# One gate's modulation computed among the FFN's products, and the residual stream loaded step by step

## The chip, the cores and the metric

The kernel runs on one core of a Trainium2 chip. The metric is the device time of one execution in microseconds (us): the median of a few executions, here 2656.18 us over three (2654.99 to 2662.91). The core has five engines with queues of their own: TensorE (PE in the profile; PEld is its loading of weights), VectorE (DVE), ScalarE (ACT), GpSimd (POOL) and SyncE (SP), which here only issues transfers. Each runs its queue in order and waits on semaphores for the others. Transfers issued by SyncE and by GpSimd go to the same 16 DMA engines.

## The reference

One layer of a hybrid decoder for 512 prompt tokens and 8 single new tokens, model width 2048, in float32. Cut to what matters:

```
mod = silu(c) @ w_ada + b_ada                       # 6 x 2048 columns
sh1, sc1, gt1, sh2, sc2, gt2 = split(mod, 6)
h = rmsnorm(x, g_norm_mix) * (1 + sc1) + sh1
q, k, v, p_rwkv = split(h @ w_in)
att = banded_attention(q, k, v)                     # window 128, ALiBi, sinks
rw, S, last = rwkv7_mix(p_rwkv, ...)                # delta-rule recurrence, 16 heads
x = x + gt1 * (concat(att, rw) @ w_out)
h2 = rmsnorm(x, g_norm_ffn) * (1 + sc2) + sh2
gate, up = split(h2 @ w_ffn_in)                     # hidden width 5632
x = x + gt2 * ((silu(gate) * up) @ w_ffn_out)
y = rmsnorm(x, g_norm_final)
```

Besides y it returns the last 128 key and value rows of the prompt, the recurrent states, the last projection row, and for the new tokens the key and value caches shifted by one row with the new row at the end. The caches hold 8 x 128 rows of 256 numbers each (1 MB a cache).

## The kernel before

**Numbers.** Activations lie transposed, features on the 128 partitions, and all 520 tokens as two halves of 260 columns. A float32 product is done as three: each weight and each activation is split into a high part that the fast matmul type holds exactly and the rest, and high x high, high x low and low x high are summed (`mm3`, line 98). Weights come in units of 128 x 512 (256 KB): SyncE issues the load (`raw`, line 86), ScalarE casts the high part (`wh`, line 88), VectorE subtracts (`wl`, line 91). In the FFN's first stage the like is done in lines 1269 and 1270.

**Stages.** (1) Startup: norm and first modulation. (2) Input projection: 39 tiles `pm`, each 16 steps of six matmuls of 260 columns, with the RWKV recurrence running between them. Of it only the chain matters here: for each pair of heads the prompt goes through 32 half-steps, each one small matmul group into `psc` from the state `Z`, then a step on VectorE and one on ScalarE that write `Z` anew, before the next can start. The pair's output follows (`pY`, its group norm, the gate `pg`, then `V` stored to `catd` in device memory). (3) Query, key and value tiles of the projection are written to device memory and read back for attention. (4) The concatenated activations are read back (`catl` from `catd`, line 1349, two buffers), split, and the output projection runs: `wout_part(0, 8)` over the first 8 of 16 steps of the contraction, which needs no attention output and makes 16 tiles `po` of 48 matmuls while attention runs between them, then `wout_part(8, 12)`, then the last four steps half by half with the second norm. (5) FFN, first stage (`ffn_in`): 44 tiles of hidden width in a scheme of seven products in place of eight (line 1439), with sums of weights made by accumulating transfers on GpSimd's queue. (6) FFN, second stage (`pf`, line 98), last norm, results (line 1602).

**Modulation.** `ada_gen` (line 304) computes the gates and shifts GT1, SH2, SC2 and GT2 while stage 2 runs. Each is 64 groups: SyncE loads 256 KB of `w_ada` into `ar` (three buffers), and TensorE multiplies it in four column tiles of 32 x 128 (line 314). After every 16 groups the result is copied by ScalarE, transposed and added to the bias.

**Order.** The order of instructions comes from two places. Background jobs are generators (`ada_gen`, the recurrence, attention, loads), and `pump()`, called after each step of six matmuls in the main tiles, advances those whose time has come in a small model clock (0.62 a call; `spent` adds what a job's own instruction takes). A scheduler then lays the instructions out on each engine.

**Residual stream.** `x_load` loads the input x again into eight tiles of two feature blocks each (`x1[0]` to `x1[7]`), on which `accumulate` (line 1193) adds GT1 times an output tile, on VectorE. `new_kv_sample` copies the 127 kept rows of the two caches from device memory to device memory on GpSimd's queue, after the first store of key rows.

Of the kernel before, what the change touches and what calls it, by code (L numbers as in the profile page):

```python
# [7 lines left out]
F32 = mybir.dt.float32  # L8
F32R = mybir.dt.float32r
AF = mybir.ActivationFunctionType  # L10
ALU = mybir.AluOpType
# [3 lines left out]
P = 128  # L15
KD = 16
T = 512
NS = 8
HB = 260
# [8 lines left out]
SH1, SC1, GT1, SH2, SC2, GT2 = 0, 16, 32, 48, 64, 80  # L28
# [35 lines left out]
class Kern:  # L64
    def __init__(self, tc, I, O, upto="all"):
        self.tc, self.nc, self.I, self.O, self.upto = tc, tc.nc, I, O, upto
        self.n = 0
        self.bg = []
        self.free, self.done_at = {}, 0.0
        self.px = PacedCore(self)  # L70
        self.nada = 0
        self.sample_done = self.kv_done = self.decode_done = False
        self.cat_out, self.cat_in = set(), 0
        self.psc = None
        self.squares, self.pending = [None, None], None

# [72 lines left out]
    def run(self):  # L149
        tc, nc, I = self.tc, self.nc, self.I  # L150
        R = dict(side="right")
        with ExitStack() as st:
# [15 lines left out]
            with ExitStack() as st2:  # L168
# [33 lines left out]
                with tc.tile_pool(name="ap", bufs=1, **R) as self.ap:  # L202
                    self.attn_phase()
                    self.wout_part(0, 8)
                    self.wout_part(8, 12)
                    self.drain()
# [97 lines left out]
    def ada_gen(self):  # L304
        nc = self.px
        for c in (GT1, SH2, SC2, GT2):
            for q in range(4):
# [508 lines left out]
    def x_load(self):  # L816
        for i in range(8):
            src = self.I["x"]
            for a, b in ((0, 1), (1, 2)) if i == 0 else ((0, 2),):
                (self.nc.sync if i else self.nc.gpsimd).dma_start(self.x1[i][:, a:b], src[:, 2 * i + a:2 * i + b])  # L820
            if i in (1, 2, 3, 5, 7):
                self.done_at += 4
                yield

# [22 lines left out]
    def kv_gen(self):  # L847
# [9 lines left out]
        for gp in range(2):  # L857
# [4 lines left out]
            yield  # L862
        self.first_kv = self.nc.gpsimd.dma_start(O["kp"], self.Kt[:, :, 384:512])
        nc.gpsimd.dma_start(O["vp"], self.Vt[:, 3])
# [3 lines left out]
    def new_kv_sample(self):  # L868
        nc, I, O, ap = self.px, self.I, self.O, self.ap
        with self.tc.issue_after(self.first_kv.ins):  # L870
            for n in ("k", "v"):
                self.nc.gpsimd.dma_start(O[n + "s"][:, 0:127, :], I["cache_" + n][:, 1:128, :])
        pt = self.aux("ptx")
# [487 lines left out]
    def wout_part(self, k0, k1):  # L1361
# [4 lines left out]
        for o in range(KD):  # L1366
            ps = self.ps_m.tile([P, 2, 512], F32, tag="m", name=self.nm("po"))
            for kk in range(n):
# [4 lines left out]
                self.pump()  # L1373
            self.accumulate(o, ps, GT1)

    def wout_half(self, h, kept):
# [23 lines left out]
    def ffn_in(self, st):  # L1400
# [45 lines left out]
        def finish(ht, pc, cu):  # L1446
# [7 lines left out]
            yield  # L1454

        norm = self.norm_second(lambda nm: mt(nm)[:, 0])
        early = len(self.pcd)
# [15 lines left out]
        for i, ht in enumerate(order):  # L1473
# [4 lines left out]
            else:  # L1478
                p12 = mt("pm")
            p45, p67, p3 = mt("pm"), mt("pm"), mt("pm")  # L1480
            for g in range(2):
                a11, a21 = load(ht, 0, 0, g), load(ht, 1, 0, g, places[(2 * i + g) % 4])
                a22 = load(ht, 1, 1, g, "raw")
# [18 lines left out]
                for ps, a, b in ((p45[:, 1], a21, T1), (p67[:, 0], a11, T2), (p67[:, 1], s3, T3),  # L1502
                                 (p45[:, 0], a22, T4), (p3[:, 0], a12, B22)):
                    product(ps, weights(a), b, g)
                    if b is T1:
                        if old and g:
                            nc.vector.tensor_tensor(s3, a11, a22, ALU.subtract)
                        nc.vector.tensor_tensor(a12, a12, a11, ALU.add)
                        next(rest, None)
# [78 lines left out]
    def last_block(self, b, g):  # L1588
# [39 lines left out]
        r = self.norm(1, mt("ssq3")[:, 0], nc)  # L1628
        for eng, o in ((nc.vector, 0), (nc.gpsimd, 8), (nc.vector, 2), (nc.gpsimd, 10), (nc.vector, 4), (nc.vector, 6),
                       (nc.gpsimd, 14), (nc.vector, 12)):  # L1630
            result(eng, 1, r, o, 2)

# [108 lines left out]
```

## Time and profile before

| | |
|---|---|
| median of 3 executions | 2656.18 us (2654.99 to 2662.91) |
| the profiled execution | 2657.76 us, of which the span 2656.0 us |
| TensorE busy | 2554.5 us, 96% of the span |
| VectorE, ScalarE, GpSimd busy | 1723.8, 1105.9, 382.5 us |
| moved by DMA | 460 MB, 173 GB/s mean |
| last projection tile ends, output projection begins | 926.7 us |
| FFN, first and second stage | the stretch 1262 to 2124 lies in the first; the second from 2130 us |

The span is what the profiler sees of one execution; the device time is a little longer. A timeline row gives start, duration, engine, line, operation, output<-input and count, and in brackets the idle time before it with what released it. A row of a group gives busy time and mean duration in ns, and then the idle time before its instructions. A row of a stretch gives its length, then busy time (and instructions) of PE, PEld, DVE, ACT and POOL, then the granted clock of TensorE (1.00 is full), the busy share of the DMA engines and GB/s. A row of transfers gives count, KB of each, and the median time from issue to landing.

### The profile page before, as it was taken

Reading aid. Unit: us, or ns where it says so; the run is one execution under the profiler, and the core shown is the slowest. Engines: PE = TensorE matmul, PEld = TensorE weight load, DVE = VectorE, ACT = ScalarE, POOL = GpSimd, SP = SyncE. Lnnn points to the kernel's source line nnn. Section 1 sums busy time; section 2 is a strip of 40 time slices with the busy share of each in tenths; the row PEclk is TensorE's granted clock in tenths of the full one; section 3 lists DMA queues with packets and bytes.
Section 4 is the critical chain, followed back from the end, with each engine's and each line's share of the span. In section 5 each row is a group of like instructions: output and inputs, shape, how many; then the busy total and the mean of one; then the engine's idle time right before and its main releaser. Section 6 shows DMA issues by size and latency. Waiting matters only on the chain. (4 is left out here: it accounts for less than half of the span.)

```text
span 2656.0 us, 59166 instructions
## 1 busy us (share of the span) xinstructions
PE 2554.5 (96%) x23373; PEld 2340.7 (88%) x23373; DVE 1723.8 (65%) x3880; ACT 1105.9 (42%) x2153; POOL 382.5 (14%) x525
## 2 busy tenths in 40 slices
PE   7899999999999999998999999999999999999997
PEld 4677777888787889898999999999999999999997
DVE  5466767777657444678777777777777763444456
ACT  3133444545533324547544444444444532222225
POOL 0012112112112000021111212111121100000004
PEclk9999999999989999999999999999999999999999
DMA  9855445455546675245777777777777552333333
GB/s 347 294 165 154 152 126 162 149 166 160 159 153 207 203 251 146 94 160 183 191 201 204 193 208 198 191 207 198 194 208 200 155 184 92 124 125 102 116 105 106
DMA packets 241704, 460.22 MB, mean 173 GB/s; under 512 B 32353, under 2 KB 44561, under 8 KB 241393
## 3 DMA queue, kind: packets, MB, share of 16 engines
q1 hardware_dynamic: 206880, 379.88, 44.5%
q0 software_dynamic: 33904, 75.50, 13.4%
q8 instruction: 183, 3.00, 0.5%
q10 hardware_dynamic: 640, 1.05, 0.2%
q14 instruction: 97, 0.79, 0.1%
HBM read 421.73 MB, written 35.59 MB: 172 GB/s over the span
## 5 line engine op out<-in xcount | busy, mean ns | idle before, releaser
L88 ACT CAST wh<-raw 128x512 fp32r<-128x512 f32 (+2 forms) x410 | 246.9, 606 | 510.5 <-PE pf L98 278.9
L98 PE MATMUL pf<-go,wh 128*128 128x260 f32 x2560 | 414.1, 281 | 0.0
L91 DVE TENSOR_TENSOR wl<-raw,wh 128x512 fp32r<-128x512 f32 (+2 forms) x410 | 283.8, 694 | 200.4 <-ACT wh L88 194.8
L98 PEld LDWEIGHTS pf<-go,wh 128*128 128x128 f32 x2560 | 354.0, 188 | 0.1
L98 PE MATMUL pm<-hH,wh 128*128 128x260 f32 (+1 forms) x1248 | 301.3, 319 | 7.3 <-ACT wh L88 6.7
L1269 ACT CAST wh<-sr 128x512 fp32r<-128x512 f32 x320 | 198.1, 621 | 261.7 <-PE pm L1439 232.0
L1270 DVE TENSOR_TENSOR wl<-sr,wh 128x512 fp32r<-128x512 f32 x320 | 220.6, 690 | 83.0 <-ACT wh L1269 75.9
L98 PE MATMUL pm<-hH,wl 128*128 128x260 f32 (+1 forms) x1248 | 265.4, 292 | 5.2 <-DVE wl L91 5.1
L98 PE MATMUL pf<-go,wl 128*128 128x260 f32 x1280 | 267.7, 282 | 0.0
L1439 PE MATMUL pm<-xT,wh 128*128 128x260 f32 x1408 | 263.2, 286 | 4.4 <-DVE pc L1516 4.3
L98 PE MATMUL pm<-hL,wh 128*128 128x260 f32 (+1 forms) x1248 | 263.4, 291 | 0.0
L1439 PE MATMUL pm<-T,wh 128*128 128x260 f32 x1408 | 257.6, 283 | 0.0
L98 PEld LDWEIGHTS pm<-hH,wh 128*128 128x128 f32 (+1 forms) x1248 | 196.5, 191 | 57.8 <-issue 31.6
L1439 PEld LDWEIGHTS pm<-xT,wh 128*128 128x128 f32 x1408 | 216.9, 188 | 11.0 <-DVE pc L1516 6.1
L1439 PEld LDWEIGHTS pm<-T,wh 128*128 128x128 f32 x1408 | 216.9, 188 | 0.0
L98 PEld LDWEIGHTS pm<-hH,wl 128*128 128x128 f32 (+1 forms) x1248 | 197.4, 192 | 16.0 <-DVE wl L91 8.7
L1439 PE MATMUL pm<-B0H,wl 128*128 128x260 f32 x704 | 201.4, 286 | 9.6 <-DVE wl L1270 9.1
L98 PEld LDWEIGHTS pm<-hL,wh 128*128 128x128 f32 (+1 forms) x1248 | 196.9, 191 | 7.5 <-issue 5.2
L1439 PE MATMUL pm<-B0H,wh 128*128 128x260 f32 x704 | 200.3, 285 | 2.0 <-DVE acct L1206 1.7
L98 PEld LDWEIGHTS pf<-go,wl 128*128 128x128 f32 x1280 | 200.9, 188 | 0.0
L1439 PE MATMUL pm<-B0L,wh 128*128 128x260 f32 x704 | 198.9, 282 | 0.0
L1439 PE MATMUL pm<-T,wl 128*128 128x260 f32 x704 | 198.7, 282 | 0.0
(427 smaller groups left out, 5243.8 us busy)
## 6 DMA issues: line engine op xcount, KB each, us to landing
ar<-in_w_ada SPq DMA_DIRECT2D x256, 256.0 KB, 3.1
sr<-in_w_fi SPq DMA_DIRECT2D x176, 256.0 KB, 4.6
raw<-in_w_fo SPq DMA_DIRECT2D x176, 256.0 KB, 2.6
raw<-in_w_in SPq DMA_DIRECT2D x144, 256.0 KB, 3.7
araw<-in_w_ada SPq DMA_DIRECT2D x64, 512.0 KB, 6.5
raw<-in_w_fi SPq DMA_DIRECT2D x120, 256.0 KB, 4.6
s<-in_w_fi SPq DMA_DIRECT2D x80, 256.0 KB, 4.4
s<-in_w_fi POOLq DMA_DIRECT2D x80, 256.0 KB, 5.1
```

The costliest lines, as they stand in the source:

```text
L88: nc.scalar.copy(wh[:, :n], raw[:, :n])
L91: nc.vector.tensor_tensor(wl[:, :n], raw[:, :n], wh[:, :n].bitcast(F32), ALU.subtract)
L98: nc.tensor.matmul(ps[:m, bank, :HB], w, a[:, k, h, :], start=first and i == 0, stop=last and i == 2, skip_group_check=True,)
L1269: nc.scalar.copy(H, src)
L1270: nc.vector.tensor_tensor(L, src, H.bitcast(F32), ALU.subtract)
L1439: nc.tensor.matmul(ps[:, :HB], x[:, s], y, start=g == k == i == 0, stop=g == 1 and k == 3 and i == 2, skip_group_check=True)
```

## The change

Four edits.

1. `ada_gen` leaves GT2 out. Its 64 groups move into the FFN's first stage: in iterations 11, 18, 25 and 32 of 44, 16 groups each, four groups after each of two products (those with T2 and T4), in both halves of the contraction, into the free bank of `p3`. The loads stand at the iteration's halves, into tiles of a pool of 12. GT2 is used in the FFN's second stage only.
2. `x_load` puts tile 0 on GpSimd's queue, tiles 1 and 2 on SyncE's, and tiles 3 to 7 on GpSimd's, each behind a copy of one element from the x tile three places before it, which waits until the output tiles of that one have been accumulated.
3. The cache copies move from the first key store to behind the last x load, by the program between `wout_part(0, 8)` and `wout_part(8, 12)`.
4. The last eight multiplies of results go all to VectorE; before, three were GpSimd's.

```diff
@@ the program @@
                     self.wout_part(0, 8)
+                    with tc.issue_after(self.last_x.ins):
+                        for n in ("k", "v"):
+                            nc.gpsimd.dma_start(self.O[n + "s"][:, 0:127, :], I["cache_" + n][:, 1:128, :])
                     self.wout_part(8, 12)
@@ ada_gen @@
-        for c in (GT1, SH2, SC2, GT2):
+        for c in (GT1, SH2, SC2):
@@ x_load @@
-                (self.nc.sync if i else self.nc.gpsimd).dma_start(self.x1[i][:, a:b], src[:, 2 * i + a:2 * i + b])
-            if i in (1, 2, 3, 5, 7):
-                self.done_at += 4
-                yield
+                self.last_x = (self.nc.sync if 0 < i < 3 else self.nc.gpsimd).dma_start(self.x1[i][:, a:b], src[:, 2 * i + a:2 * i + b])
+            if i < 2:
+                continue
+            self.done_at += 4
+            yield
+            if i < 7:
+                while self.cat_o < 2 * (i - 2) + 2:
+                    yield
+                nc = self.nc
+                nc.gpsimd.tensor_copy(self.x1[i + 1][:, 0, 0, 0:1], self.x1[i - 2][:, 1, 1, 259:260])
@@ new_kv_sample @@
-        with self.tc.issue_after(self.first_kv.ins):
-            for n in ("k", "v"):
-                self.nc.gpsimd.dma_start(self.O[n + "s"][:, 0:127, :], I["cache_" + n][:, 1:128, :])
@@ wout_part, after each output tile @@
             self.accumulate(o, ps, GT1)
+            self.cat_o += 1
@@ ffn_in @@
+        def ada(ps, q, g, j):
+
+            for k in range(8 * g + 4 * j, 8 * g + 4 * j + 4):
+                for c in range(4):
+                    nc.tensor.matmul(ps[32 * c:32 * c + 32, 0:128], self.cT[:, k, :], self.pieces[0][:, c * 128:(c + 1) * 128], start=k == 0, stop=k == KD - 1,
+                                     tile_position=(0, 32 * c), skip_group_check=True)
+                self.pieces.pop(0)
+            if k < KD - 1:
+                return
+            res = self.fp.tile([P, 2, HB], F32, tag="n", bufs=self.nb, name=self.nm("adar"))[:, 0, 0:128]
+            nc.scalar.copy(res, ps[:, 0:128])
+            nc.tensor.transpose(ps[:, 128:256], res, self.ident)
+            f0 = GT2 + 4 * q
+            nc.vector.tensor_tensor(
+                self.mod[:, f0:f0 + 4, :], ps[:, 128:256].rearrange("p (f t) -> p f t", f=4)[:, :, 0:9],
+                self.par[:, P_BA + f0:P_BA + f0 + 4].unsqueeze(2).broadcast_to([P, 4, 9]), ALU.add)
+
+        def ada_load(q, g):
+            for k in range(8 * g, 8 * g + 8):
+                t = self.fp.tile([P, 2, HB], F32, tag="n", bufs=self.nb, name=self.nm("ar"))
+                t = t.rearrange("p a t -> p (a t)")[:, 0:512]
+                nc.sync.dma_start(t, I["w_ada2"][12 + q, k])
+                self.pieces.append(t)
...
+            q = (11, 18, 25, 32).index(i) if i in (11, 18, 25, 32) else None
             for g in range(2):
+                if q is not None:
+                    ada_load(q, g)
...
                     product(ps, weights(a), b, g)
+                    if q is not None and (b is T2 or b is T4):
+                        ada(p3[:, 1], q, g, b is T4)
@@ last_block @@
-        for eng, o in ((nc.vector, 0), (nc.gpsimd, 8), (nc.vector, 2), (nc.gpsimd, 10), (nc.vector, 4), (nc.vector, 6),
-                       (nc.gpsimd, 14), (nc.vector, 12)):
-            result(eng, 1, r, o, 2)
+        for o in range(0, KD, 2):
+            result(nc.vector, 1, r, o, 2)
```

Since the background jobs go by the model clock, taking 64 groups out shifts what stands behind them. Three places of the order of instructions show it. In the changed file the lines of helpers are one to seven further down.

TensorE, at the end of the last pair's recurrence. Before, the pair's output `pY` stands among the matmuls of a projection tile, with groups of `ada` between them, and more projection tiles follow:

```order
L49 MATMUL psc<-Z_1733,LS_1738 64x64 x2
L98 MATMUL pm_11127<-hH,wh_11180 128x260 x2
L98 MATMUL pm_11127<-hL,wh_11180 128x260 x2
L98 MATMUL pm_11127<-hH,wl_11181 128x260 x2
L314 MATMUL ada_11012<-ar_11168,cT 32x128 x4
L98 MATMUL pm_11127<-hH,wh_11180 128x260 x2
L98 MATMUL pm_11127<-hL,wh_11180 128x260 x2
L98 MATMUL pm_11127<-hH,wl_11181 128x260 x2
L49 MATMUL pY_11203<-Z_1733,RR_9364 32x64 x10
L314 MATMUL ada_11012<-ar_11196,cT 32x128 x4
L49 MATMUL pY_11203<-Z_1733,RR_9364 32x64 x22
L98 MATMUL pm_11127<-hH,wh_11180 128x260 x2
```

With the change the projection tiles have run out here. The last of them ends, and the recurrence goes on alone: `psc` reads the state `Z`, `L` and `LS` are the two kinds of half-step.

```order
L99 MATMUL pm_10921<-hH,wh_11027 128x260 x2
L99 MATMUL pm_10921<-hL,wh_11027 128x260 x2
L99 MATMUL pm_10921<-hH,wl_11028 128x260 x2
L49 MATMUL psc<-Z_1733,L_1218_8537 32x64 x2
L49 MATMUL pYx_11082<-cst,ys 64x64 x2
L49 MATMUL pY_11174<-Z_1733,RR_9381 32x64 x9
L49 MATMUL psc<-Z_1733,LS_1738 64x64 x2
L49 MATMUL pY_11174<-Z_1733,RR_9381 32x64
L49 MATMUL psc<-Z_1733,L_1218_8537 32x64 x2
L49 MATMUL pY_11174<-Z_1733,RR_9381 32x64
L49 MATMUL psc<-Z_1733,LS_1738 64x64 x2
L49 MATMUL pY_11174<-Z_1733,RR_9381 32x64
```

From the first `psc` row here 24 half-steps of the pair's 32 stand one behind the other, each with a piece of `pY` in between; no projection tile is left to stand among them, and before the first `po` come only small matmuls (decode attention, `pt`, `pg`, transposes, first logits).

SyncE, around the store of the last pair's output (`catd_87`) and the loads of the concatenated activations (`catl`). Before:

```order
L49 DMA catd_87<-V_9369 128x512
L49 DMA ar_11402<-in_w_ada 128x512
L463 DMA qd_105<-sp_11366 128x512
L49 DMA ar_11424<-in_w_ada 128x512
L1349 DMA catl_11394<-catd_80 128x512
L1349 DMA catl_11416<-catd_81 128x512
L49 DMA ar_11452<-in_w_ada 128x512
L86 DMA raw_11582<-in_w_in 128x512
L86 DMA raw_11614<-in_w_in 128x512
L1349 DMA catl_11444<-catd_82 128x512
L86 DMA raw_11646<-in_w_in 128x512
L1349 DMA catl_11466<-catd_83 128x512
```

With the change:

```order
L49 DMA catd_87<-V_9386 128x512
L49 DMA q_11657<-qd_100 128x512
L49 DMA q_12014<-qd_101 128x512
L1356 DMA catl_11246<-catd_80 128x512
L1356 DMA catl_11250<-catd_81 128x512
L49 DMA q_12310<-qd_102 128x512
L49 DMA q_12599<-qd_103 128x512
L1356 DMA catl_11254<-catd_82 128x512
L1356 DMA catl_11258<-catd_83 128x512
L1356 DMA catl_11262<-catd_84 128x512
L1356 DMA catl_11266<-catd_85 128x512
L49 DMA bias_12312<-in_alibi 128x2x256
```

The store stands ahead of the `catl` loads in both. Before, `ar` and projection weights stand among them, and tiles of the projection run beside them; with the change there are neither, and the first units of `w_out` are loaded ahead of the store. Seven x loads came behind these rows on SyncE before; now five of the eight tiles stand on GpSimd's queue, the cache copies behind them.

TensorE, in the FFN's first stage, iteration 11 (`T_1` is the last operand of a product, `ar` the loaded modulation weights):

```order
L1447 MATMUL pm_18271<-T_1_14708,wh_18353 128x260 x2
L1447 MATMUL pm_18271<-T_1_14708,wl_18354 128x260
L1468 MATMUL pm_18272<-ar_18273,cT 32x128 x4
L1468 MATMUL pm_18272<-ar_18275,cT 32x128 x4
L1468 MATMUL pm_18272<-ar_18277,cT 32x128 x4
L1468 MATMUL pm_18272<-ar_18279,cT 32x128 x4
L1447 MATMUL pm_18271<-xT_14995,wh_18385 128x260 x2
L1447 MATMUL pm_18271<-xT_14995,wl_18386 128x260
```

Four groups of four small matmuls each stand between two products that stood next to each other before.

More of the change, by code (lines that the diff above doesn't have):

```diff
@@ L74, in __init__ @@
         self.psc = None
+        self.cat_o = 0
         self.squares, self.pending = [None, None], None
@@ L862, in kv_gen @@
             yield
-        self.first_kv = self.nc.gpsimd.dma_start(O["kp"], self.Kt[:, :, 384:512])
+        nc.gpsimd.dma_start(O["kp"], self.Kt[:, :, 384:512])
         nc.gpsimd.dma_start(O["vp"], self.Vt[:, 3])
@@ L869, in new_kv_sample @@
         nc, I, O, ap = self.px, self.I, self.O, self.ap
-        with self.tc.issue_after(self.first_kv.ins):
-            for n in ("k", "v"):
-                self.nc.gpsimd.dma_start(O[n + "s"][:, 0:127, :], I["cache_" + n][:, 1:128, :])
         pt = self.aux("ptx")
@@ L1454, in finish @@
             yield
+        def ada(ps, q, g, j):
[19 more added lines that the diff above has]
+                self.pieces.append(t)
+        self.pieces = []
         norm = self.norm_second(lambda nm: mt(nm)[:, 0])
```

## The prediction

> **What bounds the kernel now.** I read the page's head first, then busy time by stage, then the rows of the two places that the change touches. First the head.
>
> ```profile
> span 2656.0 us, 59166 instructions
> PE 2554.5 (96%) x23373; PEld 2340.7 (88%) x23373; DVE 1723.8 (65%) x3880; ACT 1105.9 (42%) x2153; POOL 382.5 (14%) x525
> ```
>
> TensorE is busy 96% of the span, so its own work and the few places where it waits decide. Busy time in four stretches (last columns: granted clock, DMA share, GB/s): the last part of the in-projection, the first two output-projection tiles, the attention with the tiles after them, the FFN's first stage.
>
> ```profile
> 724.00:926.80 202.80, 196.79 (x1996) 161.36 (x1995) 116.76 (x260) 68.49 (x157) 28.81 (x22) 0.96 0.60 190
> 926.80:938.30 11.50, 11.50 (x98) 11.50 (x98) 3.88 (x15) 2.25 (x4) 2.71 (x5) 1.00 0.97 295
> 938.30:992.00 53.70, 47.77 (x426) 46.01 (x426) 24.78 (x71) 15.96 (x37) 3.55 (x6) 0.94 0.68 244
> 1262.00:2124.00 862.00, 850.88 (x6978) 840.74 (x6977) 644.82 (x1118) 402.96 (x673) 163.27 (x206) 1.00 0.75 196
> ```
>
> TensorE idles 6 us in the first (first two columns), none in the second, 5.9 in the third, 11 of 862 in the fourth. Work moved into the FFN therefore costs nearly its full time, and work taken from the in-projection pays only if TensorE has something else to do there.
>
> **Removed from the in-projection.** The 64 groups of GT2 lie in the first stretch; its groups of instructions, and what TensorE waited for:
>
> ```profile
> L314 PE MATMUL ada<-ar,cT 128*32 128x128 f32 x512 | 28.3, 289 | 3.9 <-DMA ar<-in_w_ada 3.8
> L49 PE MATMUL psc<-Z,LS 128*64 128x64 f32 x124 | 10.8, 254 | 0.5 <-ACT Z L49 0.3
> ...
> L49 PE MATMUL pg<-SG,lf 128*128 128x512 f32 x12 | 4.0, 427 | 0.0
> L49 PE MATMUL pY<-Z,RR 128*32 128x64 f32 x128 | 2.7, 222 | 0.0
> ```
>
> One such group between two others:
>
> ```profile
> 708.44 0.41 PE L98 MATMUL pm<-hL,wh 128*128 128x260 f32 x2
> 708.68 0.40 PE L98 MATMUL pm<-hH,wl 128*128 128x260 f32 x2
> 709.02 0.43 PE L314 MATMUL ada<-ar,cT 128*32 128x128 f32 x8
> 709.27 0.28 PE L49 MATMUL psc<-Z,L 128*32 128x64 f32 x4
> ```
>
> A pair of projection matmuls normally takes 0.24 us (708.44 to 708.68). Here the group starts 0.34 after the pair, so 0.10 late, and holds the queue 0.25. At least 64 x 0.35 + 3.8 of waiting = 26 us goes. At most it is all busy time and idle time, 32.2, plus 64 x 0.10 = 39 us. I take 36.5, near the top, since most groups stand between projection matmuls and delay those behind them too.
>
> **What takes its place.** By the order of instructions, the projection tiles now run out with 24 of the last pair's 32 chain half-steps still to come; before, they ran between these tiles. A half-step goes TensorE, VectorE, ScalarE, TensorE; two of them (projection rows left out):
>
> ```profile
> 849.45 0.34 PE L49 MATMUL psc<-Z,LS 128*64 128x64 f32 x4
> ...
> 849.91 0.28 DVE L49 TENSOR_SCALAR Z<-psc,PC 64x64 f32<-64x64 f32 x1 [0.84 <-PE psc L49]
> ...
> 850.22 0.31 ACT L49 ACTIVATE Z<-psc,PC 64x64 f32<-64x64 f32 x1 [0.91 <-DVE Z L49]
> ...
> 850.75 0.31 PE L49 MATMUL psc<-Z,L 128*32 128x64 f32 x4
> 850.78 0.62 ACT L88 CAST wh<-raw 128x512 fp32r<-128x512 f32 x1 [0.25 <-PE pm L98]
> ...
> 851.17 0.23 DVE L49 COPY Z<-psc 32x64 f32<-32x64 f32 x1 [0.99 <-PE psc L49]
> ...
> 851.44 0.21 ACT L49 COPY Z<-psc 32x64 f32<-32x64 f32 x1
> ```
>
> The LS step ends its round at 850.53 (850.22 + 0.31) and the L step at 851.65, so 1.0 to 1.3 us each, mean near 1.13; under other work a half-step cost TensorE some 0.45 (its own 0.25 and the disturbed pairs about it). Moving 24 of them out of the stretch shortens it by 24 x 0.45 = 10.8. Some 4 us of the pair's other matmuls move too: half of the 2.7 of pY, four pg at 0.43, four pt at about the 0.3 of other matmuls. The last projection tile thus ends at 926.7 - 36.5 - 10.8 - 4 = 875.4.
>
> From there 24 x 1.25 = 30 us of chain with TensorE almost idle. I take 1.25 rather than 1.13 because of the clock. Behind tiny matmuls, and again behind a stall, it falls (third-last column):
>
> ```profile
> 778.00:784.00 6.00, 6.00 (x33) 5.00 (x33) 2.12 (x14) 1.86 (x6) 0.00 (x0) 0.50 0.33 108
> ...
> 948.00:954.00 6.00, 2.30 (x10) 2.30 (x11) 1.42 (x4) 0.62 (x1) 0.94 (x2) 0.67 1.02 410
> 954.00:960.00 6.00, 6.00 (x42) 6.00 (x41) 2.08 (x3) 2.06 (x4) 0.14 (x1) 0.77 0.73 238
> 960.00:966.00 6.00, 6.00 (x52) 6.00 (x52) 2.40 (x6) 1.49 (x3) 0.00 (x0) 1.00 0.72 230
> ```
>
> At half clock the 0.31 to 0.34 us of matmul become some 0.13 longer. The Trainium skill speaks against the change here ("TensorE: Matmul & The Clock Gate", Part 1: The HAM clock gate): the array gets half its clock after an idle window of about 3.4 us and full clock only after as long a sustained run. The 0.67 and 0.77 above agree, standing behind a stall of 4.29 us quoted below. By the rule the whole exposed chain and the first products behind it run at half clock, and 24 x 1.13 = 27 us of chain would be 30; by the rows' own pace 27.
>
> Then the pair is normalised and written; the last step, the multiply that ends it, the store, and what loads and stores take to land over the run (last column):
>
> ```profile
> 886.71 0.27 DVE L49 TENSOR_SCALAR L<-psc,PC 64x64 f32<-64x64 f32 x1 [2.22 <-PE psc L49]
> ...
> 900.54 0.69 DVE L49 TENSOR_TENSOR V<-V,pg 128x512 f32<-128x512 f32 x1 [2.04 <-PE pg L49]
> ```
> ```profile
> 901.26 0.33 SPq L49 DMA_DIRECT2D catd<-V  x1
> ```
> ```profile
> raw<-in_w_out SPq DMA_DIRECT2D x68, 256.0 KB, 3.2
> ...
> catl<-catd SPq DMA_DIRECT2D x16, 256.0 KB, 3.3
> ...
> catd<-V SPq DMA_DIRECT2D x8, 256.0 KB, 2.2
> ```
>
> That tail took 14.5 us (886.71 to 901.23), much of it in queue behind the casts and subtractions of projection weights, none of which is left; I take 9.5, ends 7.5 and 14.5. The store of the last pair stands ahead of all eight loads of the concatenated activations on SyncE's queue, so none of them starts early, and two buffers let two be under way. Store 0.3 + 2.2; each pair of loads 0.3 to issue, 3.3 to land and some 0.6 for its cast (a cast of this size took 0.62 at 850.78), 4.2 for a round and four rounds: 875.4 + 30 + 9.5 + 2.5 + 16.8 = 934.2, and the last products of two tiles, now worked k by k in turns, end some 2 us on, at 936.2. Before, two tiles were done at 938.3. **Term: -2 us**, ends -14 and +10.
>
> **The output projection.** Two stalls stand in the third stretch, and beside them the transfers issued just ahead:
>
> ```profile
> 941.12 0.93 PE L49 MATMUL ptx<-cst,vf 128*128 128x128 f32 x7
> ...
> 943.69 0.51 PE L98 MATMUL po<-cH,wh 128*128 128x260 f32 x2 [1.64 <-ACT wh L88]
> ...
> 951.70 0.80 PE L98 MATMUL po<-cH,wh 128*128 128x260 f32 x2 [4.29 <-ACT wh L88]
> ```
> ```profile
> x<-in_x SPq DMA_DIRECT2D x6, 520.0 KB, 12.5
> raw<-in_w_out SPq DMA_DIRECT2D x4, 256.0 KB, 11.9
> ```
>
> Weights took 11.9 us to land between residual loads of 12.5, where over the run such weights take 3.2. In the change, most x tiles come step by step on GpSimd's queue and the cache copies (2 MB) stand behind the last of them, so SyncE carries weights. I take both stalls as gone, -5.9, with the cold clock behind them: 10 matmuls in 2.30 and 42 in 6.00 us, where a pair in 0.24 makes it 1.2 and 5.0, so -2.1. Twelve transposes, a dozen logits' matmuls and 16 for the decode rows now run inside the wait for the chain or for the loads; at 0.93 / 7 = 0.13 or little less each, -4. **Term: -12**, ends -14 and -3 (a stall may move behind the next x load or the copies, which land in about 10 us).
>
> **The FFN.** The 16 calls of 4 groups stand between products, back to back. The nearest row is the startup's four groups of twice the width:
>
> ```profile
> 21.33 1.93 PE L273 MATMUL psc<-araw,cT 128*32 128x256 f32 x32
> ```
>
> 1.93 / 4 / 2 = 0.24 us per group at most; I take 0.22, since a row's time runs past the start of the next. A call is 4 x 0.22 + some 0.35 at its two edges (0.10 late ahead of it as above, the rest for the fall back to full products) = 1.25; 16 of them 20 us, and four transposes with their edges 0.5 each: 22 us. Lower end 16 x 0.9 + 1 = 16 (no edges); upper end 64 x 0.5 = 32 (the price of the removed ones: 36.5 less 3.8 of waiting, over 64, is 0.51). ScalarE's four copies are covered by the next iteration's products, which the order puts ahead of the transpose; uncovered they would cost 4 x 0.5. What TensorE waits for in this stage today:
>
> ```profile
> PE pm L1439 <- DVE wl L1270: 6.2, 14, 1.1
> ```
>
> VectorE is the late one, so a call can absorb a wait right behind it: at most one or two per call-bearing iteration, 4 of 44, -1 in all. The loads add 4 bursts of 16 x 256 KB; a burst of 4.2 MB within some 30 us puts 140 GB/s on top of 196, in all more than the 295 that went with a share of 0.97 and less than the 410 with 1.02. I take +0, since the order issues these loads two iterations (2 x 862 / 44 = 39 us) ahead; ends 0 and +8, a burst's excess at each of four. **Term: +21**, ends +15 and +40.
>
> **The end.** Critical row and last group:
>
> ```profile
> 2644.42 0.70 DVE x L1602
> ...
> 2646.82 4.00 DVE x L1602 x3
> ```
>
> Before, VectorE ends at 2650.8; eight multiplies alone at 0.70 end at 2644.4 + 5.6 = 2650.0. **Term: -1**, ends -1.5 and +1.
>
> **Sum.** -2 - 12 + 21 - 1 = +6 on 2657.76, the profiled run, or 2663.8. That run is 1.6 above the median of 2656.18, which leaves **2662 us**. A measurement here tells 0.3%, or 8 us, from no change: under 2648.2 is faster, over 2664.1 slower.
>
> **Rivals.** (1) *The FFN has no room* (slower). The groups cost what they cost alone, 32 + 2 for the transposes, 12 over my term, and the bursts starve the weights a little, +3: 2677. It decides once a group costs over 0.27 us, edges counted apart. For it: 11 idle us in 862. Against it: the back-to-back row. (2) *The exposed chain is longer* (slower). Half-steps of 1.4, +3.6; a tail of 12, +2.5; the first two tiles, at half clock, set the pace in place of the loads, 8 k of 2 x 6 matmuls at 0.24 = 23 us for 17, +6: 2674. Against it: after the stall the clock is at 1.00 within some 9 us (960 to 966). (3) *The chain runs at its rows' pace* (faster). 1.05 per half-step with free engines, -5; tail 7.5, -2; loads landing nearer the stores' 2.2, -3; the removed groups worth 39, -2.5; FFN calls with half the edges, -3: 2646. For it: ScalarE and VectorE have nothing else to do there. (4) *The stalls stay*: x tiles come just in time, the weights are late behind other loads, and the 8 us of the second term's stalls and clock remain: 2670.
>
> **Chances.** Forecast 0.42, alone 2647 to 2671; of this 0.02 falls under 2648.2 and 0.10 over 2664.1. Rival 1 0.14, rival 2 0.11, rival 3 0.28, rival 4 0.05. Faster 0.28 + 0.02 = 0.30; slower 0.14 + 0.11 + 0.05 + 0.10 = 0.40; same 0.30. The range that leaves a tenth out on each side is 2641 to 2684, cutting into rival 3 below and past rival 1 above with part of its burst.
>
> **What would show it.** Between about 875 and 915 us TensorE should show only psc and pY rows, 1.1 to 1.4 us apart, with a clock near 0.5 to 0.6; no wait of po on wh over 1 us; the third stretch's work done some 14 us before 992; the FFN some 21 us longer, with its waits on wl no larger. Wrong would be: a chain of over 40 us, x-tile waits on VectorE ahead of the accumulations, or sr waits in the four iterations.

## The result, and the profile after

The changed kernel takes 2683.51 us (median of 4, 2678.89 to 2688.13); the kernel before, beside it, 2655.59 (4 runs, 2651.89 to 2662.91). The ratio is 1.0102, 95% interval 1.0073 to 1.0130: slower by 27 us. The forecast was 2662, in a range of 2641 to 2684; the time lies half a us inside that range's upper end, two of the four executions lie above it, and it falls in the "slower" that had 0.40.

The page of the kernel after, its head, busy times and granted clock in 40 slices:

```profile
span 2680.3 us, 59182 instructions
PE 2553.0 (95%) x23373; PEld 2347.2 (88%) x23373; DVE 1720.9 (64%) x3883; ACT 1105.9 (41%) x2153; POOL 383.0 (14%) x532
PEclk9999999999999698999999999999999999999999
```

TensorE's busy time is 1.5 us less than before and the span 24.3 longer, so TensorE stands idle for longer. The fourteenth slice (from 871 to 938) has a clock of 0.6. The stretches of it that answer to the four of before:

```profile
724.00:876.90 152.90, 146.37 (x1289) 135.79 (x1288) 99.22 (x209) 53.63 (x114) 25.89 (x18) 0.97 0.37 126
876.90:923.60 46.70, 29.10 (x229) 17.13 (x228) 14.68 (x57) 11.20 (x34) 9.71 (x14) 0.57 0.66 194
...
945.00:992.00 47.00, 47.00 (x387) 45.90 (x385) 22.67 (x66) 10.38 (x17) 2.71 (x7) 1.00 0.43 141
992.00:1100.00 108.00, 101.46 (x902) 89.95 (x900) 53.03 (x193) 47.64 (x141) 5.45 (x8) 0.92 0.45 139
...
1207.00:2153.00 946.00, 926.42 (x7913) 909.15 (x7914) 694.74 (x1209) 442.65 (x756) 170.67 (x220) 1.00 0.77 209
```

The in-projection ends 50 us earlier (876.9 for 926.7). Then follow 46.7 us in which TensorE shows 29 us of busy time at a clock of 0.57. No wait is left from 945 to 992; 6.5 us of idle time come in the next stretch. The FFN's first stage (the last of these rows) is 946 us, for 921 before.

The same run by landmarks (start of a stage's first instruction, or the last of 48 matmuls per output tile counted through the timeline's po rows):

| | before | after | lead of after |
|---|---|---|---|
| last projection tile starts its last pair | 926.5 | 876.9 | 49.6 |
| two output tiles done | 938.0 | 942.2 | -4.2 |
| ten | 1002.0 | 993.0 | 9.0 |
| twelve | 1026.6 | 1025.1 | 1.5 |
| FFN's first stage begins | 1209.4 | 1207.6 | 1.8 |
| its second stage begins | 2130.2 | 2153.2 | -23.0 |
| last sum of squares | 2641.0 | 2666.6 | -25.6 |
| end of the span | 2656.0 | 2680.3 | -24.3 |

So there are three places: a lead of 49.6 us is spent by the second tile; a lead of 9 is lost between ten and twelve tiles; and the FFN takes 24.8 us more in its first stage and 2.5 more in its second. The end gives 1.3 back.

**First place.** TensorE's timeline in the gap, the first, four later and the last half-step, and then the first `po`:

```profile
877.19 0.31 PE L49 MATMUL psc<-Z,L 128*32 128x64 f32 x4
...
879.70 0.30 PE L49 MATMUL psc<-Z,L 128*32 128x64 f32 x4 [0.57 <-ACT Z L49]
...
881.77 0.31 PE L49 MATMUL psc<-Z,L 128*32 128x64 f32 x4 [0.57 <-ACT Z L49]
...
883.84 0.43 PE L49 MATMUL psc<-Z,L 128*32 128x64 f32 x4 [0.46 <-ACT Z L49]
...
888.63 0.43 PE L49 MATMUL psc<-Z,L 128*32 128x64 f32 x4 [0.44 <-ACT Z L49]
...
907.35 0.48 PE L49 MATMUL psc<-Z,LS 128*64 128x64 f32 x4
...
923.65 1.23 PE L99 MATMUL po<-cH,wh 128*128 128x260 f32 x4
```

The chain alone is 24 half-steps in 31 us. A small matmul group takes 0.30 at first and 0.43 from 883.84 on, 6 to 7 us behind the last projection tile. A pair of half-steps takes 2.07 us before that (879.70, then 881.77) and 2.45 after it (888.63, then 891.08). Once, the chain has a hole of some 2.3 us: its step on VectorE stands behind copies of another job, which wait for a transfer there.

```profile
886.16 0.52 DVE L49 COPY rstd<-QW 64x16 f32<-64x16 f32 x4 [2.72 <-DMA QW<-QS]
```

Behind the chain SyncE issues:

```profile
916.74 0.33 SPq L49 DMA_DIRECT2D catd<-V  x1
917.11 0.92 SPq L49 DMA_DIRECT2D q<-qd  x2
918.83 0.79 SPq L1356 DMA_DIRECT2D catl<-catd  x2
919.73 5.33 SPq L49 DMA_DIRECT2D q<-qd  x2
925.19 6.18 SPq L1356 DMA_DIRECT2D catl<-catd  x4
...
935.96 0.93 SPq L1356 DMA_DIRECT2D catl<-catd  x2
```

Between the first pair of loads and the next stand two loads of queries, 5.3 us; the second waits for a buffer that is held until a store of new key rows (`kst`) has landed, 4.3 us.

**Second place.** TensorE's wait, ScalarE's behind it, and the transfers from 1000 to 1013:

```profile
1015.31 0.90 PE L49 MATMUL pt<-cst,Lg 128*128 128x128 f32 x3 [6.45 <-DVE sm L49]
```
```profile
1013.05 0.62 ACT L144 CAST cH<-catl 128x512 fp32r<-128x512 f32 x1 [6.85 <-DMA catl<-catd]
```
```profile
catd<-q SPq DMA_DIRECT2D x1, 256.0 KB, 9.6
```
and such stores over the whole run before:
```profile
catd<-q SPq DMA_DIRECT2D x8, 256.0 KB, 2.0
```
and GpSimd's issues just ahead:
```profile
995.86 0.60 POOL L208 DMA_DIRECT2D out_ks<-in_cache_k  x1
996.45 0.57 POOL L208 DMA_DIRECT2D out_vs<-in_cache_v  x1
```
and what these took to land:
```profile
out_ks<-in_cache_k POOLq DMA_DIRECT2D x1, 1016.0 KB, 8.9
out_vs<-in_cache_v POOLq DMA_DIRECT2D x1, 1016.0 KB, 11.8
```

The wait is put down to VectorE's `sm`. VectorE and ScalarE had stood idle, ScalarE behind a load of the first attention output, and that load behind its store, which took 9.6 us to land where such stores took 2.0 before. The two cache copies had been issued some 5 us ahead of it, and three loads of the old value cache (256 KB each, 11 us to land) stand between.

**Third place.** A call in the FFN, and the worst wait:

```profile
1484.68 0.28 PE L1447 MATMUL pm<-T,wl 128*128 128x260 f32 x1
1484.89 1.08 PE L1468 MATMUL pm<-ar,cT 128*32 128x128 f32 x32
1485.90 0.50 PE L1447 MATMUL pm<-xT,wh 128*128 128x260 f32 x2
1486.24 0.28 PE L1447 MATMUL pm<-xT,wl 128*128 128x260 f32 x1
...
1525.64 0.80 PE L1447 MATMUL pm<-xT,wh 128*128 128x260 f32 x2 [4.47 <-DVE pc L1554]
```

A call starts 0.09 late (0.21 after a matmul that alone takes 0.12), holds TensorE 1.01, and the pair behind it takes 0.34 in place of 0.24: 1.20 us, 16 times 19 us. The 4.47 us wait is for a step of VectorE on the tile `pc`. VectorE had itself stood still until then: ahead of that step in its queue stands a sum that needs a loaded FFN weight, `sr`, and SyncE had issued that load among the gate's.

```profile
1512.78 3.38 SPq L1485 DMA_DIRECT2D ar<-in_w_ada  x5
...
1517.21 0.33 SPq L1433 DMA_DIRECT2D sr<-in_w_fi  x1
...
1524.55 0.69 DVE L1537 TENSOR_TENSOR sr<-sq,sr 128x512 f32<-128x512 f32 x1 [4.54 <-DMA sr<-in_w_fi]
1525.16 0.42 DVE L1554 TENSOR_TENSOR pc<-pm,pc 128x260 f32<-128x260 f32 x1
```

This `sr` took 7.2 us to land, where such loads take 4.5 over the run. Twelve of the gate's loads are issued from 1499 to 1516, as soon as the calls at 1485 to 1501 have freed their tiles; the calls that need them begin at 1636. Before, TensorE's waits on `pc` in this stage were (total, count, longest):

```profile
PE pm L1439 <- DVE pc L1516: 4.3, 7, 1.7
```

### The profile page after: what moved, and what is told of

The parts are those of the page before. It is cut to its first block, busy times and chain, and to the rows that moved or that the text cites. A ratio compares the mean times of both kernels' runs of the same rounds, so it can differ in the third digit from the quotient of the medians.

```text
span 2680.3 us, 59182 instructions
## 1 busy us (share of the span) xinstructions
PE 2553.0 (95%) x23373; PEld 2347.2 (88%) x23373; DVE 1720.9 (64%) x3883; ACT 1105.9 (41%) x2153; POOL 383.0 (14%) x532
## 5 line engine op out<-in xcount | busy, mean ns | idle before, releaser
L99 PE MATMUL pm<-hH,wh 128*128 128x260 f32 (+1 forms) x1248 | 295.0, 315 | 6.8 <-ACT wh L89 6.2
L99 PE MATMUL pm<-hH,wl 128*128 128x260 f32 (+1 forms) x1248 | 259.7, 288 | 5.5 <-DVE wl L92 5.3
```

The source lines that it names most:

```text
L99: nc.tensor.matmul(ps[:m, bank, :HB], w, a[:, k, h, :], start=first and i == 0, stop=last and i == 2, skip_group_check=True,)
```

## The experiments

Each was timed in turns with the kernel before on its own chip, so ratios are compared, not times; the change's own ratio is the 1.0102 above (1.0073 to 1.0130). On the three chips of these runs the kernel before took 2662 to 2664 us. Landmarks are read from one execution each. How far they scatter shows where the order is the same: the last projection tile starts its last pair at 876.9 in the change, and at 875.0, 882.9 and 883.1 in three kernels below that differ from it in the FFN alone.

### The chain covered by projection tiles

```diff
@@ main_tile @@
-            self.pump()
+            self.pump(0.75)
```

The model clock runs faster against the projection's matmuls, and so the background jobs are given out more densely.

> The change, with one number altered: the model clock advances 0.75 instead of 0.62 per step of a projection tile, so that by the order of instructions the last pair's chain ends with 121 projection rows still behind it, and no half-step stands alone. Theory A (the 46.7 us between the last projection tile at 876.9 and the first po at 923.7 were waiting on the exposed chain, its tail and its store; only some 21 us of matmuls lie in them): 24 to 30 us faster than the change, 2654 to 2660 us, TensorE busy over 90% from 850 to 940. Rival B (the recurrence has its own latency, so a denser chain only puts the waits among the tiles): under 10 us faster, 2674 or more, with waits of psc on ScalarE's Z rising by as much as the gap shrinks.

Measured: 0.998 of the time before (0.996 to 1.000), 1.2% less than the change, about 32 us with some 9 of uncertainty. TensorE passes from the projection to the output projection with nothing between them:

```profile
903.81 0.40 PE L99 MATMUL pm<-hH,wl 128*128 128x260 f32 x2
904.05 0.40 PE L99 MATMUL po<-cH,wh 128*128 128x260 f32 x2
```

Theory A holds in the time: what the exposed chain cost is of the size of the whole loss. In the landmarks the gain is 22 us at two tiles (920.0 for 942.2) and 11 at the start of the FFN: half of it is given back in the attention, on the way to the sixteenth tile. The last projection tile ends at 904 (897 in a later run of the same order), where 877 + 24 x 0.45 + 4 = 892 was to be expected. Whether the faster model clock would also help the kernel before was not run, so what the cover alone is worth, apart from the denser order of all other jobs, stays open.

### The copies put back

```diff
-                    with tc.issue_after(self.last_x.ins):
-                        for n in ("k", "v"): ...                   # ahead of wout_part(8, 12)
+        with self.tc.issue_after(self.first_kv.ins):
+            for n in ("k", "v"): ...                               # new_kv_sample
```

> The change with the two cache copies put back behind the first key store. Theory A (the 6.45 us that pt waits at 1015 come from the copies, issued at 996, which hold up the store of an attention output, 9.6 us to land, and the load of it behind): that wait falls under 1 us and the time by some 5 us, to 2676 to 2681, part of it lost again to copies that now run beside the loads of the concatenated activations at 920 to 940. Rival B (other loads, the value cache's and the last x tile, do that): the wait stays, 2682 to 2686.

Measured: 1.015 (1.0121 to 1.018), slower than the change. Neither theory had this. The edit does not stay in its place: the scheduler now lays a first round of attention ahead of the first `po`, which starts 53 us later than in the change. TensorE there:

```profile
975.98 0.57 PE L49 MATMUL psc<-PTs,rstd 128*64 128x2 f32 x4
976.48 1.23 PE L99 MATMUL po<-cH,wh 128*128 128x260 f32 x4
```

and the longest wait from 905 to 980 is ScalarE's for VectorE in that attention:

```profile
ACT sm L49 <- DVE sm L49: 18.3, 2, 11.9
```

So the run says nothing on the copies' price; it says that putting them back there, behind an exposed chain, also moved attention ahead of the output projection.

### The FFN without the gate, and with one piece in place of 64

```diff
@@ without the gate @@
-                if q is not None:
-                    ada_load(q, g)
-                    if q is not None and (b is T2 or b is T4):
-                        ada(p3[:, 1], q, g, b is T4)
+        nc.vector.memset(self.mod[:, GT2:GT2 + 16, :], 0.5)
@@ one piece @@
-            for k in range(8 * g, 8 * g + 8):       # 64 loads
+            for k in range(1):                      # only at g == 0: 4 loads, kept for all 16 groups
```

> The change with the 64 groups and their loads left out of the FFN's first stage; GT2 is a constant instead, so this modulation is not computed. Theory A (16 calls of 1.2 us and four transposes, plus waits on pc that the loads cause and a late first weight of the second stage): 25 to 27 us faster than the change, 2657 to 2659, with the FFN's first stage at about 921 us as before. Rival B (only the matmuls count, the waits are of the stage itself): 19 to 21 us faster, 2663 to 2665.

> The change with one loaded piece used for all 16 groups of a quarter, so 4 loads of 256 KB in place of 64; GT2's values are not those of the reference. All matmuls stay. Theory A (the bursts of loads delay pc and the second stage's first weights): the longest wait on pc falls from 4.5 us to under 1.5, and the time by 4 to 6 us, to 2678. Rival B (TensorE's shift against VectorE makes the waits): within 2 us of the change.

Measured: 1.0012 (0.9996 to 1.0027) without the gate, 1.0063 (1.0045 to 1.0081) with one piece. So the gate costs 0.9% in the FFN, about 24 us with some 9 of uncertainty, which lies between the ranges of the first run's two theories and rules neither out. Its loads are a share of that: 0.39% by these ratios, 10 us with some 9 of uncertainty, and by the landmarks 4.3 us in the first stage (941.3 for 945.6). Without the gate the first stage took 925.3, not the 921 of theory A. TensorE's waits on `pc` in the first stage (total, count, longest), of the change, without the gate, with one piece:

```profile
PE pm L1447 <- DVE pc L1554: 9.1, 8, 4.5
```
```profile
PE pm L1447 <- DVE pc L1551: 6.7, 8, 1.9
```
```profile
PE pm L1447 <- DVE pc L1555: 5.3, 8, 1.8
```

Without the loads the long one is gone while the matmuls stay, as theory A of the second run has it, though at 1.8 us and not under the 1.5 that it gave.

### The edits apart

The gate's move alone (`x_load`, the copies and the last multiplies as before), and the other three without it (GT2 back in `ada_gen`, nothing in the FFN):

> The first edit alone: the gate's modulation in the FFN, everything else as before. In the order of instructions the exposed chain is there again, and behind it a first round of attention stands ahead of the first po, as in the kernel with the copies put back (1.015). Theory A (the gate's move by itself costs some 25 us in the FFN and gains nothing ahead of it, since the chain and then attention run at their own pace): 1.013 to 1.018 of the time before. Rival B (x loads at once let po run early and the move alone is no worse than the whole change): 1.006 to 1.011.

> The other three edits without the first: GT2 stays in the in-projection, x loads come step by step, the copies behind the last, the multiplies on VectorE. By the order no half-step is exposed. Theory A (these edits take away the two waits of po on wh, 5.9 us, their cold clock, 2 us, and 1 us at the end, and cost up to 6 us where the copies now meet attention's loads): 0.996 to 0.999 of the time before. Rival B (attention's own pace decides how early the output projection ends, so nothing is gained): 0.9995 to 1.002.

Measured: 1.017 (1.0146 to 1.0194) and 1.000 (0.9979 to 1.0021). The gate's move alone is worse than the whole change, in the range of theory A; its first `po` stands at 974.1, behind attention, as with the copies put back. The other three by themselves are worth nothing that can be told. TensorE's waits in that kernel from 926 to 1060:

```profile
PE pt L49 <- DVE sm L49: 5.9, 1, 5.9
PE po L99 <- ACT wh L89: 1.3, 1, 1.3
```

Before, `po` waited 5.9 us on `wh` here; that falls to 1.3 (2.0 in the whole span), and the wait behind the copies takes its place. The time is in the range of rival B, that attention's pace takes the gain back. The trace has both terms of theory A, and the second, given as "up to" 6, is 5.9 and takes back what the first gains. Which of the two holds the time at 1.000 this run can't tell.

### The copies elsewhere

The copies issued at the start of the FFN's second stage in the program, once with the chain covered and once in the change itself:

```diff
-                    with tc.issue_after(self.last_x.ins): ...
+        for n in ("k", "v"):                        # last_block, ahead of the first unit
+            nc.gpsimd.dma_start(self.O[n + "s"][:, 0:127, :], I["cache_" + n][:, 1:128, :])
```

> The kernel with the covered chain (0.998), and the cache copies issued at the start of the FFN's second stage. TensorE's, ScalarE's and VectorE's order is that of the covered-chain kernel. Theory A (the wait of pt on sm behind the copies, 5.9 us there, goes and nothing else comes): 0.9945 to 0.9965 of the time before. Rival B (the attention jobs are late anyhow, and the wait comes back as another one): 0.997 to 0.999.

> The change with only the two cache copies moved to the start of the FFN's second stage; every engine but GpSimd has the same order as in the change. Theory A (the 6.45 us wait of pt on sm near 1015 comes from the copies): wait under 1 us, 5 to 8 us faster than the change, so 1.007 to 1.0085 of the time before. Rival B (attention's pace holds TensorE there): within 2 us of the change, 1.0095 or more.

Measured: 1.0002 (0.9983 to 1.0021) and 1.0089 (1.0058 to 1.0119). The copies did not go where the program has them: nothing held them back, and both kernels issue them at 1.6 us, at the very start. The startup is limited by transfers (347 GB/s in the first slice of before, at a share of 0.9 or more), and the third projection tile is done some 10 us later than in the kernels they are compared with (128 for 118, 130 for 119). The wait itself is a clean test, since all engines but GpSimd keep their order; of `pt`, from 941 to 1060 in the second, and the stores of attention outputs from 1005 to 1045:

```profile
PE pt L49 <- DVE sm L49: 0.2, 1, 0.2
```
```profile
catd<-q SPq DMA_DIRECT2D x2, 256.0 KB, 2.6
```

From 6.45 to 0.2 us, and ten to twelve tiles take 25.6 us for 32.1 in the change; the store lands in 2.6 us for 9.6. The loads of the old value cache are still there, so the wait came from the copies. What that is worth in the whole time these two can't tell.

Queued behind the last store of the FFN's first stage they stay there (with the chain covered, as in the first run):

```diff
+        with self.tc.issue_after(self.last_gd.ins):
+            for n in ("k", "v"): ...
```

> The covered-chain kernel (0.998) with the cache copies queued on GpSimd behind the last store of the FFN's first stage, which pins them there (in the two kernels before, the order had put them at the very start). Theory A (the 5.9 us wait of pt on sm is the copies' and nothing takes its place): 0.9945 to 0.9965 of the time before. Rival B (attention's jobs have slack that takes the gain back by the end of the output projection): 0.997 to 0.999.

Measured: 0.9977 (0.9959 to 0.9995), for 0.998 with the copies in their place. The wait is gone (ten to twelve tiles in 24.3 us for 31.9), and by the landmarks the FFN starts 280.0 us after the last projection tile, for 292.4. The time shows less than the 6 us of theory A: it lies in the range of rival B, but the gain of 0.03% has an interval of about 0.25% either way, so neither theory is settled by it.

### The gate's loads spread

Two loads at each half of the three iterations ahead, and four in the iteration's second half, each behind that half's last weight load:

```diff
-                if q is not None:
-                    ada_load(q, g)                  # 8 at once
+                for j, i0 in enumerate((11, 18, 25, 32)):
+                    if i in (i0 - 3, i0 - 2, i0 - 1):
+                        with self.tc.issue_after(self.last_ld.ins):
+                            ada_load(j, 4 * (i - i0 + 3) + 2 * g, 2)
+                    elif i == i0 and g: ...         # the last 4
```

> The change with only the gate's 64 loads spread two by two over the three iterations ahead; only SyncE's order differs. Theory A (the bursts delay pc and the second stage's first weight): longest wait on pc under 1.9 us and 4 to 7 us off the FFN, 1.0075 to 1.0088 of the time before. Rival B (any 16 MB more cost the same, burst or not): within 2 us of the change, 1.0095 or more.

Measured: 1.0089 (1.0068 to 1.0110), with only SyncE's order changed. The wait in the first stage:

```profile
PE pm L1447 <- DVE pc L1559: 6.9, 7, 2.4
```

The longest falls from 4.5 to 2.4 us, short of the "under 1.9" of theory A; the first stage takes 940.3 us for 945.6, the second 510.4 for 513.4. By the landmarks 8 us, by the time 3.5 with some 9 of uncertainty: the ratio lies between the two ranges, and the time settles neither.

### The three repairs together

The copies pinned, the loads spread, and the chain covered by a faster model clock that is set only late: 1.2 from the start of the decode recurrence, or 1.0 from the end of the loop over pairs.

```diff
@@ main_tile @@
-            self.pump()
+            self.pump(self.pace)                    # 0.62 at first
@@ the program @@
                     last = self.rwkv_phase()
+                    self.pace = 1.0                 # or 1.2, ahead of self.start(self.rwkv_sample())
```

> The change with three repairs: the model clock advances 1.2 per step only in the projection's last part, from the decode recurrence's start on, so that the chain is covered (66 projection rows behind it) and the earlier part keeps its pace; the copies pinned behind the FFN's first stage; the gate's loads two by two over three iterations ahead in place of bursts. Theory A (the early part of the covered-chain kernel lost some 12 us to waits that its denser steps made; the copies are worth 6, the loads 5): 0.989 to 0.993 of the time before. Rival B (the chain's steps wait for each other wherever they stand): 0.994 or more.

> As the kernel with the late pace, but the clock advances 1.0 from the end of the loop over pairs on, somewhat earlier and less, so that 121 projection rows stand behind the chain. Theory A: 0.989 to 0.993 as well, with less waiting of psc on Z and the first po without a gap. Rival B (rows left behind the chain count, not the pace): faster than the late pace by over 0.2%.

Measured: 0.9967 (0.9954 to 0.9980) and 0.9952 (0.9933 to 0.9970). Both beat the kernel before, the second by 0.5%, about 13 us, and the change by 1.5%. They fall short of the 0.989 to 0.993 of theory A and lie in the range of the first run's rival B (0.994 or more). The 0.15% between them is less than their uncertainty, so the second run's rival B is not shown. The last projection tile ends at 896 to 897 in both, as in the second run with 0.75 throughout, and not at 892, so the early pace was not what held the first run back. The second one's stretches, from ahead of the last projection tile to the FFN:

```profile
860.00:896.00 36.00, 35.70 (x347) 34.36 (x348) 17.45 (x32) 13.69 (x28) 1.85 (x2) 1.00 0.46 150
896.00:992.00 96.00, 92.63 (x851) 87.57 (x851) 51.64 (x168) 35.70 (x92) 11.71 (x22) 0.96 0.69 210
992.00:1176.00 184.00, 176.11 (x1452) 160.10 (x1450) 116.67 (x373) 93.48 (x233) 22.50 (x38) 0.97 0.41 124
1176.00:2120.00 944.00, 926.62 (x7917) 908.86 (x7918) 695.42 (x1209) 442.54 (x757) 171.74 (x222) 1.00 0.78 212
```

TensorE is busy throughout ahead of 896; then some 11 us of idle time remain in the stages behind it, and the FFN's first stage is hardly shorter than in the change (943.3 us), though its loads are spread.

Taken over all runs the burst's price is small and blurred. The first stage takes 944 to 950 us in the seven kernels with bursts, 940.3 to 944.5 in the three with the loads spread, 941.3 with one piece, and 920.8 to 925.3 in the three without the gate there. The longest wait on `pc` tells them apart: 3.6 to 5.2 us with bursts, 1.6 to 2.5 in all others. The second stage does not: it takes 510 to 514 us with the loads spread and 510 to 513 with bursts.

## Why the prediction was right or wrong

The direction with the largest chance and the range held, the range by half a us, which is luck; the forecast case, +6 us, did not. By its terms, in the profiled execution:

- **End of the projection, 875.4.** 877.2 measured (876.86 and its 0.4). The removed groups at 36.5 us, the 24 half-steps at 0.45 and the 4 us of the pair's other matmuls hold as a sum; no run tells them apart, and the same order gave 875 to 883 in other executions, so that it came within 2 us is partly luck.
- **The exposed chain, 30 us, and the tail, 9.5.** 31 us and 8.8 (907.95, the last step on VectorE, to 916.7, the store). The cold half-step was right too: 1.03 us warm, 1.23 cold. But not all were cold, and the sum came out because VectorE's hole of 2.3 us, no term of the forecast, made up the difference. The clock was 0.57 over the gap, and by the rows' durations it fell 6 to 7 us after the last projection tile, while the longest idle time of TensorE up to then was 0.57 us. The rule of the Trainium skill that the prediction weighed ("TensorE: Matmul & The Clock Gate", Part 1: The HAM clock gate) puts half clock behind an idle window of about 3.4 us. The trace agrees as far as the clock fell where the large matmuls had ended, but no such idle window stands ahead of the fall.
- **The eight loads, 16.8 us in rounds of 4.2.** This step failed: two tiles were done at 942.2, forecast 936.2. The rounds were 5.2, 6.3 and 4.2 apart in their casts: two query loads, one of which waits for a buffer, stand in SyncE's queue between the first pairs; a buffer comes free only behind VectorE's subtraction, for which SyncE waited 4.5 us in the four rounds; and other steps of ScalarE stand ahead of the third pair's casts. The query loads stood in the order shown; I had priced the `catl` loads and their casts alone. The term is +4 in place of -2, inside its ends.
- **The output projection, -12.** Right up to ten tiles: 50.8 us from the second to the tenth, for 64.0 before, so -13.2. Then 7.5 came back between the tenth and the twelfth. The sentence that failed is the one that let the copies "stand behind the last of them, so SyncE carries weights": moved behind the last x load they met the first attention output's store and load, and a wait of 6.45 us took the place of the two of 5.9. With the copies elsewhere the wait is gone (0.2). I had it only as an end of the term, -3, and the net is about -6.
- **The FFN, +21.** +24.8. The matmuls were sized rightly, 16 calls of 1.20, 19 us for 20, though a group cost 0.25 for 0.22 and the edges 0.19 for 0.35. The burst, taken as 0 with an end of +8, is the miss: TensorE waits 4.8 us more on `pc` than before. The reason for 0 did not hold: the loads were not issued two iterations ahead of their use but as soon as tiles were free, and delayed the weights' loads beside them, VectorE's sum of `sr` and so `pc`. The forecast had looked at TensorE's waits on `wl` alone, which did not grow, and one of its own signs of being wrong, a wait for `sr`, came in the iteration behind the first calls. The +2.5 in the second stage was no term at all, and its cause stays open.
- **The end, -1.** -1.3.

In sum +4 - 13 + 7.5 - 0.3 + 25 + 2.5 - 1.3 = +24 for +6: 6 us from the rounds of loads, 6 from the copies, 4 from the FFN's first stage, the bursts above all, and 2.5 from the second stage. No rival as written came about. Rival 1 had the bursts, but with a dearer group, and groups did not cost over 0.27. Rival 2's half-steps of 1.4 did not come. The misses whose cause is known are mostly of one kind: transfers that wait for each other or for a buffer, each of which I had set at its undisturbed price.

One thing the prediction didn't ask: why 24 half-steps were left over. By the program, each of the 64 groups had also advanced the model clock by which the chain's steps are given out (by 0.3, in `ada_gen`), so without them the same chain was spread thinner over the tiles that were left; no run changes that advance by itself. One number in that clock covers the chain again and gives back 1.2%. In that light the first edit costs at least as much where the groups came from as in the FFN, where it was to be paid: 0.9% is about what the FFN costs, and 1.2% what the uncovered chain does, each with some 0.3% of uncertainty.

## What to carry to other kernels

Work that stands between the steps of a latency-bound chain is also its cover and, where a pacing model lays out the order, its clock: before it is taken away, count what is left to stand there, and set the pace anew. A transfer that is moved to "later" needs a place that is named and held, and the loads and stores at that place need to be read: here the same 2 MB made a wait of 6 us behind the x loads, delayed the startup by some 10 when issued at the start, and in a third place went with another order of everything behind them. A wait is traced through the engine that it names to what that engine waited for: here from `pc` to the load of a weight. Small edits to a program whose order a scheduler makes can't be priced one by one: the gate's move alone was 1.7%, the other three 0.0%, and the whole 1.0%.

## What the runs showed of the hardware

TensorE's granted clock fell with the exposed chain although TensorE had not stood idle for more than 0.57 us at a time until then: rows of 0.30 us became 0.43, and the mean over 46.7 us was 0.57 at 62% busy time. Two cache copies of 1 MB from device memory to device memory, themselves 8.9 and 11.8 us, made a 256 KB store beside them take 9.6 us to land; with the copies elsewhere such stores landed in 2.6. With six loads of 256 KB issued in the 7 us ahead of it, a weight's load took 7.2 us to land, where 4.5 is the median of such loads over the run.
